# A decoder layer on one core: earlier loads, earlier fetches and a buffer ring for kept results alone in the seven-product part of the feed-forward projection

## The chip, the cores and the metric

The kernel runs on one core of a Trainium2 chip. The metric is the device time in microseconds (us) of one execution. Times of single instructions come from one profiled execution.

## The reference

The reference computes one hybrid decoder layer on 2048 tokens of width 1024 in float32: a combined projection, windowed attention and a convolution side by side, an output projection, and a SwiGLU feed-forward part with 2816 inner columns. Only the last part is touched by the change:

```python
h = h + rms_norm(mixed, mix_post_g)
hn = rms_norm(h, ffn_pre_g)
ff = (jax.nn.silu(hn @ w_gate) * (hn @ w_up)) @ w_down
h = h + rms_norm(ff, ffn_post_g)
```

## The kernel before

**Stages.** The 2048 tokens are cut into four tiles of 512. Letters after an @ in the profile name the stage: A the combined projection, B attention, C the convolution taps and their normalisation, U a folded weight, W the output projection, H the turned and split operands of the feed-forward part, F the gate and up projections, G the down projection and what belongs to it. F and G take two token tiles at once, so each runs twice, first for tiles 0 and 1 and then for 2 and 3. The order is: stage_pre (F), stage_p1 (F), stage_p2 (G), and the same again.

**Split operands.** A float32 product is made of three matmuls: each operand is split into a high part, which ScalarE copies in a rounded type (split_f, L824), and a low part, which VectorE (or GpSimd for some products of the second pass) gets by subtraction (lo). The third combination, low by low, is left out.

**Seven products.** For every pair of 128 inner columns the weight has four blocks A11, A12, A21, A22 (two weight rows of 128 x 1024, each cut in two), and the activations have four blocks B (two halves of the depth by two token tiles). Instead of eight block products the kernel makes seven, with sums of blocks (the list STEPS): number 0 is A11 by B11, 1 is S1 by T1, 2 is S2 by T2, 3 is A12 by B21, 4 is S3 by T3, 5 is S4 by B22, 6 is A22 by T4. A product is 12 matmuls of 128x128 by 128x512. The sums S1 to S4 are made from the weight blocks on VectorE in the function sums; T1 to T4 are made once by stage_h_sums. In the profile the operands of the first pass are named: T1 mid and mb, T2 ql, T3 p, T4 yt and mid, B22 hl.

**Kept results.** stage_pre makes products 0 and 3 ahead for the first PRES weight rows (20 of 22 in the first pass, 16 in the second) and puts product 0 into the DRAM tensor keeps. For such a row stage_p1 makes only products 1, 2, 4, 5 and 6, and adds product 2 onto the kept result: fetch (L1038) loads it into a tile of ring gb, and a ScalarE copy, the seed, (L1066) puts it into the bank "B".

**stage_p1.** It goes over 22 weight rows m (gate and up in turn), and in each over the products j = 0, 1, ... of that row (five or seven, nst in all). For every product it first splits the weight operand of the product three further on (AHEAD = 3), then makes the product, then empties the bank: product 1 is copied to the tile y5 (L1077) and product 2 to x2 (L1080), while their banks go on being added to. After product 4, y5 gets the bank "B" added by VectorE; after product 5, x2 gets the bank of product 5. For a gate row ScalarE then makes Silu of each (L1087); for an up row VectorE multiplies the gate's result by it, and the blocks and sums of blocks are stored in the DRAM tensor mids (L1094, L1100, L1103). At the end of a product's turn, at given j, stand the steps that the change moves: sums of the next row, fetch of the next row's kept result, and loads of the row after that, which loads one weight row into ring raw (L1006) and one into ring chl (L1008), 512 KB each.

**Rings.** A tile comes from a ring of a few buffers that goes by its tag (BUFS): gb has 2, at 2, raw 2, chl 5, fa 4, w 6. A new tile waits until the buffer's earlier tile has been read for the last time. In chl a row needs three tiles: its second weight row and two for S1 to S4. Ring at is also used by stage_p2 of the first pass for its first two operands (L1169).

**Order.** The text gives each instruction a priority by its place. A planner with its own estimates of time orders each engine's list, and SP's list of transfers, by what is ready and then by priority, and hands out the buffers; so an instruction can stand well ahead of its place in the text. Once planned, each list is executed in its order, and an instruction that waits holds what is behind it. Beside stage_p1 of the first pass run the w_down sums (stage_tsums: rings wx and fc, tensor td, lines L1119 and L1125) and the convolution taps.

## Time and profile before

| | |
|---|---|
| median of 3 runs | 1996.32 us (1993.41 to 1996.72) |
| the profiled execution | 1994.08 us, of which the span from first to last instruction is 1992.1 us |
| TensorE matmul busy | 1936.4 us (97%) |
| VectorE, ScalarE, GpSimd busy | 1467.2, 953.5, 247.2 us |
| moved by DMA | 444.06 MB, mean 223 GB/s |

Engines are named PE (matmul), PEld (weight load), DVE (VectorE), ACT (ScalarE), POOL (GpSimd), and SPq (SyncE's list of transfers). In a timeline row stand start, duration, engine, line, operation, out<-in, and in brackets how long the engine was idle before it and what ended that. Line 94 (L94) is the helper that records most VectorE operations and L85 the one that records matmuls, so these are told apart by their tiles.

### The profile page before, as it was taken

To read this page: it belongs to the slowest core of one execution; us is meant where nothing else is said; L and a number is where in the kernel's file an instruction comes from. 1 tells how busy PE (TensorE), PEld (TensorE's weight loads), DVE (VectorE), ACT (ScalarE), POOL (GpSimd) and SP (SyncE) were. 2 spreads that over 40 slices of the span, in tenths; PEclk is the share of its full clock that TensorE was granted. 3 is DMA by queue.
4 is the path that set the end of the run, shared out by engine and by line. 5 is a ranking of instruction groups with operands and counts; after the bars stand their busy time and mean duration, and the time that the engine had idled before them with its cause. 6 is when DMAs were issued, how large, how long until landed. Compare 5 with 4: busy or idle time off the path is not lost.

```text
span 1992.1 us, 26622 instructions
## 1 busy us (share of the span) xinstructions
PE 1936.4 (97%) x8730; PEld 1550.4 (78%) x8730; DVE 1467.2 (74%) x2648; ACT 953.5 (48%) x1878; POOL 247.2 (12%) x339
## 2 busy tenths in 40 slices
PE   8999999999998999899999999998899999999997
PEld 6877777777776878678888788886788888888886
DVE  4999969995875899777659964667766765455557
ACT  5455354447546533234355464656543433345443
POOL 4011111101121000000000110000023332311003
PEclk9999999999999999999999999999999999999999
DMA  8786657566659767865478787759845542466664
GB/s 307 252 305 218 210 187 257 182 214 216 225 199 322 258 222 254 280 231 190 143 238 273 255 270 243 253 201 376 289 147 170 169 159 85 142 227 197 211 195 143
DMA packets 224810, 444.06 MB, mean 223 GB/s; under 512 B 22136, under 2 KB 47904, under 8 KB 224672
## 3 DMA queue, kind: packets, MB, share of 16 engines
q1 hardware_dynamic: 212768, 429.79, 64.8%
q10 hardware_dynamic: 11904, 12.59, 1.8%
q8 instruction: 68, 1.11, 0.2%
q14 instruction: 70, 0.57, 0.1%
HBM read 327.46 MB, written 114.83 MB: 222 GB/s over the span
## 4 chain that ended last, share of the span: by engine, by line
PE 77%; DMA 11%; DVE 6%; issue 2%; ACT 2%; POOL 1%; SPq 1%; DVEq 0%; POOLq 0%; ACTq 0%
PE mm@F L85 29%; PE mm@G L85 18%; PE mm@A L85 14%; PE mm@W L85 5%; PE tr@B L85 4%; PE tr@W L85 3%; DMA gb@F<-keeps 1%; DMA chl@F<-w_gate 1%; DMA raw@F<-w_gate 1%; PE mm@U L85 1%; DMA chl@G<-h_scr 1%; DVE fc@C L94 1%; DVE w@F L94 1%; DMA td<-fc@G 1%; PE tr@B L492 1%
## 5 line engine op out<-in xcount | busy, mean ns | idle before, releaser
L94 DVE SCALAR_TENSOR_TENSOR fc@C<-glu@C,colt,fc@C 128x512 f32<-128x512 f32 x480 | 357.1, 758 | 2.8
L85 PE MATMUL mm@F<-hl@H,w@F 128*128 128x512 f32 x1056 | 256.8, 394 | 8.1 <-ACT mm@F L954 8.1
L85 PEld LDWEIGHTS mm@F<-hl@H,w@F 128*128 128x128 f32 x1056 | 200.4, 190 | 51.5 <-ACT mm@F L954 9.5
L85 PE MATMUL mm@G<-hl@G,hl@G 128*128 128x512 f32 x924 | 228.0, 392 | 1.8 <-DVE hl@G L94 1.6
L85 PE MATMUL mm@A<-hl@A,w@A 128*128 128x512 f32 x840 | 209.4, 397 | 4.4 <-ACT w@A L127 1.8
L85 PEld LDWEIGHTS mm@G<-hl@G,hl@G 128*128 128x128 f32 x924 | 171.7, 188 | 38.9 <-DVE hl@G L94 2.4
L824 ACT ACTIVATE w@F<-chl@F 128x512 fp32r<-128x512 f32 x220 | 134.8, 624 | 138.9 <-PE mm@F L85 131.4
L85 PE MATMUL mm@G<-w@G,hl@G 128*128 128x512 f32 x876 | 199.4, 389 | 0.0
L85 PEld LDWEIGHTS mm@G<-w@G,hl@G 128*128 128x128 f32 x876 | 164.4, 188 | 34.1
L85 PEld LDWEIGHTS mm@A<-hl@A,w@A 128*128 128x128 f32 x840 | 156.6, 189 | 43.1 <-issue 3.1
L94 DVE TENSOR_TENSOR w@F<-chl@F,w@F 128x512 fp32r<-128x512 f32 x198 | 145.6, 739 | 37.9 <-ACT w@F L824 37.3
L85 PE MATMUL mm@F<-mid@H,w@F 128*128 128x512 f32 x528 | 137.4, 408 | 12.5 <-ACT mm@F L954 10.6
L85 PE MATMUL mm@F<-ql@H,w@F 128*128 128x512 f32 x528 | 128.5, 391 | 6.8 <-ACT mm@F L1066 4.8
L85 PE MATMUL mm@F<-p@H,w@F 128*128 128x512 f32 x528 | 132.5, 397 | 0.0
L85 PEld LDWEIGHTS mm@F<-mid@H,w@F 128*128 128x128 f32 x528 | 103.7, 198 | 36.8 <-ACT mm@F L954 11.9
L85 PE MATMUL mm@F<-x@H,w@F 128*128 128x512 f32 x528 | 126.7, 391 | 0.0
L85 PEld LDWEIGHTS mm@F<-ql@H,w@F 128*128 128x128 f32 x528 | 98.9, 188 | 29.3 <-ACT mm@F L1066 6.2
L85 PEld LDWEIGHTS mm@F<-p@H,w@F 128*128 128x128 f32 x528 | 101.7, 193 | 21.8 <-ACT at@F L1080 0.2
L85 PEld LDWEIGHTS mm@F<-x@H,w@F 128*128 128x128 f32 x528 | 98.4, 188 | 21.1 <-issue 0.8
L127 ACT ACTIVATE w@A<-raw@A 128x512 fp32r<-128x512 f32 x110 | 67.5, 626 | 92.3 <-PE mm@A L85 63.5
L94 DVE TENSOR_TENSOR w@G<-raw@G,w@G 128x512 fp32r<-128x512 f32 x73 | 52.1, 714 | 68.8 <-ACT w@G L824 67.7
L495 POOL TENSOR_SCALAR_AFFINE_SELECT p@B<-p@B 128x512 f32<-128x512 f32 x62 | 52.9, 863 | 361.2 <-ACT p@B L493 359.8
(302 smaller groups left out, 3224.8 us busy)
## 6 DMA issues: line engine op xcount, KB each, us to landing
mids<-fa@F SPq DMA_DIRECT2D x154, 256.0 KB, 2.6
raw@A<-w_in SPq DMA_DIRECT2D x55, 512.0 KB, 4.5
w@A<-lo_in SPq DMA_DIRECT2D x84, 256.0 KB, 3.5
fc@G<-mids SPq DMA_DIRECT2D x77, 256.0 KB, 3.5
fa@G<-mids SPq DMA_DIRECT2D x75, 256.0 KB, 4.2
gb@F<-keeps SPq DMA_DIRECT2D x72, 256.0 KB, 4.5
w@W<-fold SPq DMA_DIRECT2D x32, 512.0 KB, 5.3
chl@F<-w_gate SPq DMA_DIRECT2D x22, 512.0 KB, 4.0
```

Source lines behind the costliest of these rows:

```text
L85: r = nc.tensor.matmul(*args, **kw)
L94: r = op(*args, **kw)
L127: act(w[:, 0], raw, AF.Copy)
L492: nc.tensor.transpose(o[:, i * P : (i + 1) * P], pr[:, 4 * g + i], ident)
L495: nc.gpsimd.affine_select(out=pg[:, kb].rearrange("p (i q) -> p i q", q=P), in_=pg[:, 1].rearrange("p (i q) -> p i q", q=P), compare_op=AL ...
L824: act(w[:, 0], x, AF.Copy)
```

## The change

Three edits in stage_p1. The tile y5 of product 1 comes from ring at instead of gb, so that gb holds kept results only, and y5 and x2 share the two buffers of at. The fetch of the next row's kept result moves from behind product j = nst - 2 to j = nst - 4, ahead of the sums of the next row. The loads of the row after the next move from the last product, j = nst - 1, to j = nst - 3. No instruction is added or taken away.

```diff
             elif i == 1:
-                y5 = f2("gb")
+                y5 = f2("at")
                 act(y5, o, AF.Copy)
...
             if j == nst - 4:
+                fetch(m + 1)
                 sums(m + 1)
-            if j == nst - 2:
-                fetch(m + 1)
-            if j == nst - 1:
+            if j == nst - 3:
                 loads(m + 2)
             yield 2.76
```

## The prediction

> **What bounds the kernel now.** I read the page first, then the busy time by stretch, the waits, and the timelines of single engines.

> ```profile
> span 1992.1 us, 26622 instructions
> PE 77%; DMA 11%; DVE 6%; issue 2%; ACT 2%; POOL 1%; SPq 1%; DVEq 0%; POOLq 0%; ACTq 0%
> ```

> The chain that ended last is TensorE for 77% and DMA for 11%: time can be won only where TensorE waits. The seven-product part (stage_p1) runs twice, from about 682 to 1022 us and from about 1439 to 1770 us. Its stretches, and within the first the four whose clock is below 1 (columns: PE, PEld, DVE, ACT, POOL busy, PEclk, DMA share, GB/s):

> ```profile
> 682.20:880.00 197.80, 184.13 (x769) 148.53 (x768) 167.57 (x271) 67.16 (x121) 0.00 (x0) 0.96 0.75 252
> 880.00:1005.68 125.68, 125.68 (x558) 104.03 (x556) 91.88 (x145) 50.82 (x90) 0.00 (x0) 1.00 0.51 163
> 1439.00:1767.00 328.00, 328.00 (x1449) 271.60 (x1448) 198.52 (x259) 129.12 (x229) 95.88 (x67) 1.00 0.44 146
> 696.00:706.00 10.00, 8.12 (x27) 6.19 (x28) 9.29 (x15) 4.26 (x9) 0.00 (x0) 0.83 0.81 258
> 829.00:836.00 7.00, 4.79 (x15) 3.62 (x14) 6.59 (x11) 0.00 (x0) 0.00 (x0) 0.76 0.89 284
> 838.00:847.00 9.00, 7.12 (x25) 5.26 (x24) 8.36 (x14) 3.31 (x6) 0.00 (x0) 0.81 0.71 261
> 870.00:882.00 12.00, 7.48 (x23) 5.75 (x22) 9.80 (x17) 2.79 (x5) 0.00 (x0) 0.72 0.71 259
> ```

> The second pass has no idle TensorE at all, nor has the first after 880 us: nothing is to be won there. From 682 to 880 us TensorE idles 197.80 - 184.13 = 13.7 us. It also loses clock after four of the gaps; window length times (1 - PEclk) gives 1.7, 1.7, 1.7 and 3.4, together 8.5 us. The whole pot is 22.2 us. Who ends the waits in that stretch (us in total, times, longest):

> ```profile
> PE mm@F L85 <- DVE gb@F L94: 5.0, 3, 2.2
> PE mm@F L85 <- ACT mm@F L1066: 4.8, 2, 4.5
> PE mm@F L85 <- ACT w@F L824: 1.9, 1, 1.9
> PE mm@F L85 <- ACT fa@F L1087: 1.0, 1, 1.0
> PE mm@F L85 <- DVE fa@F L94: 0.9, 1, 0.9
> ACT mm@F L1066 <- DMA gb@F<-keeps: 55.9, 11, 11.7
> DVE chl@F L94 <- DMA chl@F<-w_gate: 7.7, 5, 2.7
> DVE chl@F L94 <- DMA chl@F<-w_up: 7.4, 4, 4.1
> DVE wx@G L94 <- issue: 4.8, 3, 2.3
> DVE wx@G L94 <- DMA fc@G<-w_down: 4.5, 4, 1.8
> DVE wx@G L94 <- DMA wx@G<-w_down: 3.9, 2, 2.7
> ```

> ScalarE stands 55.9 us before the seed (L1066, which copies a kept result into a bank) because the kept result has not landed. VectorE stands 15.1 us for weight rows (chl) and 13.2 us for the w_down sums that run beside this stage. TensorE's 13.6 us split into 7.7 behind ScalarE and 5.9 behind VectorE.

> **The change, part by part.** First, what sets the issue of the moved transfers today:

> ```profile
> 882.01 0.63 ACT L1087 ACTIVATE fa@F<-gb@F 128x512 f32<-128x512 f32 x1 [0.69 <-DVE gb@F L94]
> 883.02 0.38 SPq L1038 DMA_DIRECT2D gb@F<-keeps  x1
> 857.57 0.60 ACT L1066 ACTIVATE mm@F<-gb@F 128x512 f32<-128x512 f32 x1 [2.47 <-DMA gb@F<-keeps]
> 895.33 0.33 SPq L1008 DMA_DIRECT2D chl@F<-w_gate  x1
> 896.64 0.60 ACT L1077 ACTIVATE gb@F<-mm@F 128x512 f32<-128x512 f32 x1 [2.02 <-PE mm@F L85]
> SPq L1008 <- DVE w@F L94: 8.8, 7, 3.6
> SPq L1006 <- DVE chl@F L94: 7.1, 10, 1.4
> ```

> *Ring of their own (gain).* The fetch for m = 14 is issued at 883.02, when the Silu at 882.01 has read the last of y5 of m = 12: kept results and y5 share the two buffers of gb, so a fetch waits for a y5. With gb to themselves, kept 14 needs only the buffer of kept 12, free once seed 12 (857.57) has run, at 858.2. The planner took 883.02 right behind its buffer, so I expect it to take the new place as early: up to 25 us sooner, where the longest wait for one was 11.7. I take all waits behind ScalarE as gone: 4.8 + 1.9 + 1.0 = 7.7 us of idle time (the ScalarE split at 841 and the Silu at 823 were late because they stand behind a waiting seed in ScalarE's order), and the clock lost after two of them, 1.7 (838:847) and 3.4 (870:882). Gain 12.8 us. What is late next is VectorE.

> [...]

> *Fetch two products earlier in the text.* On SP it moves ahead of a finished block's store (L1094) and of the block sums (L1100, L1103). The planner already issues out of the text's order, so with the buffer free this adds nothing of its own: 0. If it lands the fetch ahead of a store in SP's list, that store is late by one issue, 0.38 us, and nobody on the chain reads it before the next stage.

> *Weight rows two products sooner (about nothing).* The chl half of row m = 16 is issued at 895.33, about where y5 of m = 14 is copied (896.64), that is at j = 0 of m = 14, while the text puts it at j = 4; the new text says j = 2. It is already ahead of both. What holds it is its buffer: the L1008 and L1006 rows wait for VectorE to finish with an old tile (8.8 and 7.1 us). Five chl and two raw buffers remain, so the issue stays where it is. Indirectly it comes sooner: the VectorE split that frees the buffer follows a ScalarE split, which no longer stands behind a late seed. Of VectorE's part of the pot (5.9 idle plus clock 1.7 for 696:706 and 1.7 for 829:836, 9.3 in all) about half follows chl (15.1 of 28.3 us of its waits) and half w_down, which the change does not touch. I take 2 (bounds 0 and 9.3).

> *y5 moves into at, beside x2 (cost).* Two buffers now hold both, so y5 of m needs y5 or x2 of m - 1 read out. The trace of before has no such wait; its bound is how far each y5 copy came ahead of the first of those last reads. There are nine such copies in the first pass; first, last, and the one that matters:

> ```profile
> 697.01 0.58 ACT L1077 ACTIVATE gb@F<-mm@F 128x512 f32<-128x512 f32 x1
> 700.92 0.63 ACT L1087 ACTIVATE fa@F<-gb@F 128x512 f32<-128x512 f32 x1 [2.81 <-DVE gb@F L94]
> 965.09 0.60 ACT L1077 ACTIVATE gb@F<-mm@F 128x512 f32<-128x512 f32 x1 [0.32 <-PE mm@F L85]
> 966.10 0.62 ACT L1087 ACTIVATE fa@F<-gb@F 128x512 f32<-128x512 f32 x1
> 782.90 0.60 ACT L1077 ACTIVATE gb@F<-mm@F 128x512 f32<-128x512 f32 x1 [0.33 <-PE mm@F L85]
> 785.48 0.64 ACT L1087 ACTIVATE fa@F<-gb@F 128x512 f32<-128x512 f32 x1 [1.46 <-DVE gb@F L94]
> 784.91 2.88 PE L85 MATMUL mm@F<-hl@H,w@F 128*128 128x512 f32 x12
> ```

> The delays run from 701.55 - 697.01 = 4.5 us (first) to 966.72 - 965.09 = 1.6 (last); the nine add up to 28.2 us. Behind the copy stand later splits on ScalarE, and the S4 product (operand hl) on TensorE, which adds onto the bank that y5 is copied from. In eight of the nine the previous row's A22 product stands in between, which itself waits for that y5 sum, and S4 starts after the delayed copy would end. In the ninth the copy would end at 786.12 + 0.60 = 786.7, S4 began at 784.91: 1.8 us. I take 1.8; bounds 0 and 28.2. In the second pass TensorE has no gap to begin with and the order of these reads is the same: 0, with another 1.8 us (one late copy in a pass) as its bound.

> *The hand-over to the down projection (cost).* stage_p2 puts its first two operands into at as well:

> ```profile
> 1006.30 0.38 SPq L1169 DMA_DIRECT2D at@G<-mids  x1
> 1014.07 1.52 PE L85 MATMUL mm@G<-hl@G,hl@G 128*128 128x512 f32 x6
> 1015.42 2.43 PE L85 MATMUL tr@W<-w@W,ql@W 128*128 128x512 f32 x10
> 1017.03 0.69 DVE L94 TENSOR_TENSOR hl@G<-at@G,hl@G 128x512 fp32r<-128x512 f32 x1 [4.80 <-ACT hl@G L824]
> 1019.43 0.68 DVE L94 TENSOR_TENSOR fa@F<-fa@F,gb@F 128x512 f32<-128x512 f32 x1
> DMA to landing us min/median/max: 3.9/4.3/4.7
> ```

> Today they load from 1006.30 through the one buffer that x2 leaves. Afterwards the last y5 and x2 hold both, until 1020.1 in the old order, or 4.8 us sooner, 1015.3, since the y5 sum stood behind VectorE's wait of 4.80 for that very operand. With 4.3 to land and one split (0.63 by the ScalarE rows, 0.69 on VectorE) the first product of stage_p2 starts at 1020.9 to 1025.7 instead of 1014.07. To fill 1014 to then TensorE has the last row's A22 product (2.7) and the output projection's products beside it, ten of them in the row of 1015.42. Bounds 0 and 9 us (nothing but A22 to run); I take 2, as products of the output projection were ready there.

> **Sum.** 12.8 + 2 - 1.8 - 2 = 11.0 us. The profiled execution took 1994.08 us (2.0 around its span), so 1983.1; it lies 2.2 us below the median of the runs shown, 1996.32, which makes 1985.3, told as 1985.

> **The rivals.** *Given back:* the seeds are on time, but VectorE's waits for w_down (13.2 us) and the hand-over at its upper bound take the place. 12.8 - 1.8 - 9 = 2.0: 1994. For it: VectorE is busy 167.57 of 197.80 us, so little slack is left there. Against: nothing says that the output projection stops just then.

> *Slower, by the shared at ring:* the order is planned anew, and where the S4 product comes ahead of the previous A22 product, as at 784.91, each y5 delay reaches TensorE, through ScalarE's later splits too. If all 28.2 do: -14.8 + 28.2 + 2 = +15.4, or 2012; half of them is +1.3. It decides, with over 4 us lost, from about 17 of the 28 us on. Against: eight of nine are covered now, and the reads that delay y5 come sooner when VectorE waits less.

> *The transfers don't move:* if a fetch stays where it was in SP's list, behind waiting stores, nothing is won, and y5 and the hand-over cost 3.8: 2000. For it: SP's list is full between 682 and 880 us (DMA share 0.75). Against: the 883.02 issue follows its buffer at once.

> **How the numbers follow.** A measurement of this kernel tells about 0.2%, 4 us, from no change. I give the forecast 0.60, its own range being 1977 (VectorE's part mostly gained, no cost) to 1991 (half of the gain). Given back and unmoved transfers get 0.19, nearly all within 4 us, the slower rival 0.21, since a newly planned order has many places to go wrong. Faster is 0.62, same 0.17, slower 0.21. The range has to reach into the slower case, up to 2004: about 0.1 lies above it and less below 1977.

> **What would show it.** ScalarE's wait for keeps at L1066 falls from 55.9 us to under 10; each L1038 is issued at least 8 us ahead of its seed; TensorE's idle time from the start of stage_p1 to the end of the w_down sums falls from 13.7 to 4 to 6 us and the clock stays at 1 except once or twice; L1008 still waits for VectorE and keeps its place; the first at@G load follows the last y5 read. It would be wrong if L1077 waits for many microseconds in total and TensorE behind it, if a gap of over 4 us opens before the first product of stage_p2, or if the seeds still wait.

## The result, and the profile after

| | before | after |
|---|---|---|
| median | 1996.37 us (1993.41 to 1999.60, 7 runs) | 1988.14 us (1985.28 to 1992.01, 7 runs) |
| the profiled execution | 1994.08 us | 1987.34 us |
| its span | 1992.1 us | 1985.6 us |

The ratio is 0.996, 95% interval 0.9949 to 0.9971: the changed kernel is 8 us faster. The forecast was 1985. From the page of the changed kernel, its span and its chain; then, from the busy time by stretch, the same three stretches of stage_p1 (columns as before):

```profile
span 1985.6 us, 26616 instructions
...
PE 74%; DMA 12%; DVE 9%; issue 2%; ACT 2%; POOL 1%; SPq 0%; DVEq 0%; POOLq 0%; ACTq 0%
```

```profile
682.20:880.00 197.80, 185.33 (x807) 150.51 (x807) 173.88 (x282) 73.08 (x128) 0.00 (x0) 1.00 0.78 261
880.00:1005.68 125.68, 125.68 (x558) 104.12 (x557) 90.36 (x142) 51.13 (x91) 0.00 (x0) 1.00 0.51 166
1439.00:1767.00 328.00, 328.00 (x1448) 271.70 (x1447) 202.78 (x257) 127.95 (x225) 96.86 (x67) 1.00 0.44 149
```

In the first stretch TensorE makes 807 matmuls where it made 769, but its busy time hardly grew: it still idles 197.80 - 185.33 = 12.5 us, and the granted clock is 1.00 instead of 0.96. The chain shows VectorE with 9% instead of 6%. Who ends the waits in that stretch (us in total, times, longest):

```profile
ACT mm@F L1066 <- DMA gb@F<-keeps: 1.0, 1, 1.0
ACT mm@F L1066 <- DVE at@F L94: 43.1, 11, 8.4
PE mm@F L85 <- DVE at@F L94: 8.1, 5, 3.0
PE mm@F L85 <- DVE fa@F L94: 4.3, 2, 3.0
ACT at@F L1077 <- DVE fa@F L94: 2.6, 2, 1.9
ACT at@F L1080 <- DVE fa@F L94: 5.2, 5, 1.7
```

The seed's wait for its kept result is gone (55.9 to 1.0 us). In its place the seed waits 43.1 us for VectorE's sums, which empty banks. TensorE waits for nobody but VectorE. In the timeline, two of its gaps with what stands before them on VectorE:

```profile
827.10 0.69 DVE L94 TENSOR_TENSOR wx@G<-fc@G,wx@G 128x512 f32<-128x512 f32 x1 [3.50 <-DMA fc@G<-w_down]
827.71 0.68 DVE L94 TENSOR_TENSOR at@F<-at@F,mm@F 128x512 f32<-128x512 f32 x1
828.44 1.66 PE L85 MATMUL mm@F<-yt@H,w@F 128*128 128x512 f32 x6 [2.97 <-DVE at@F L94]
...
867.32 0.69 DVE L94 TENSOR_TENSOR chl@F<-chl@F 128x512 f32<-128x512 f32 x1 [2.42 <-DMA chl@F<-w_gate]
870.00 1.66 PE L85 MATMUL mm@F<-mid@H,w@F 128*128 128x512 f32 x6 [3.03 <-DVE fa@F L94]
```

VectorE stands 3.50 us for a w_down block, or 2.42 us for a weight row, and the sum or product that would free TensorE's bank is queued behind that.

To see where the time came from I cut each trace at three products: the first S1 by T1 product (operand mb) and the last A22 product (operand yt) of the first pass, and the first A22 product of the second. The first pass took 334.12 us before and 325.07 after, a difference of 9.05. From there to the second pass it is 435.29 and 435.80, the second pass 318.01 in both, the tail 219.75 and 219.49. Ahead of the first pass, where the change touches nothing, the profiled run of after happened to be 2.3 us slower. So in these two runs the whole gain is in the first pass.

### The profile page after: what moved, and what is told of

Its sections match the earlier page's. It is cut to its first block, busy times and chain, and to the rows that moved or that the text cites. A ratio compares the mean times of both kernels' runs of the same rounds, so it can differ in the third digit from the quotient of the medians.

```text
span 1985.6 us, 26616 instructions
## 1 busy us (share of the span) xinstructions
PE 1930.0 (97%) x8730; PEld 1546.9 (78%) x8730; DVE 1468.7 (74%) x2648; ACT 957.5 (48%) x1878; POOL 245.1 (12%) x339
## 4 chain that ended last, share of the span: by engine, by line
PE 74%; DMA 12%; DVE 9%; issue 2%; ACT 2%; POOL 1%; SPq 0%; DVEq 0%; POOLq 0%; ACTq 0%
PE mm@F L85 29%; PE mm@G L85 16%; PE mm@A L85 14%; PE mm@W L85 5%; PE tr@B L85 4%; PE tr@W L85 2%; DVE fc@C L94 2%; PE mm@U L85 1%; DVE w@F L94 1%; DVE chl@F L94 1%; DMA raw@F<-w_gate 1%; DMA raw@F<-w_up 1%; DMA td<-wx@G 1%; PE tr@B L492 1%; DMA chl@G<-h_scr 1%
## 5 line engine op out<-in xcount | busy, mean ns | idle before, releaser
L94 DVE SCALAR_TENSOR_TENSOR fc@C<-glu@C,colt,fc@C 128x512 f32<-128x512 f32 x480 | 357.2, 758 | 2.8
L85 PE MATMUL mm@F<-hl@H,w@F 128*128 128x512 f32 x1056 | 257.7, 396 | 7.9 <-ACT mm@F L954 7.9
L85 PEld LDWEIGHTS mm@F<-hl@H,w@F 128*128 128x128 f32 x1056 | 201.2, 191 | 51.4 <-ACT mm@F L954 9.2
L85 PE MATMUL mm@G<-hl@G,hl@G 128*128 128x512 f32 x924 | 227.4, 393 | 1.9 <-DVE hl@G L94 1.9
L824 ACT ACTIVATE w@F<-chl@F 128x512 fp32r<-128x512 f32 x220 | 135.8, 625 | 166.4 <-PE mm@F L85 161.3
L85 PE MATMUL mm@A<-hl@A,w@A 128*128 128x512 f32 x840 | 208.0, 395 | 5.4 <-ACT w@A L127 2.6
L85 PEld LDWEIGHTS mm@G<-hl@G,hl@G 128*128 128x128 f32 x924 | 171.7, 188 | 38.3 <-DVE hl@G L94 2.7
L85 PE MATMUL mm@G<-w@G,hl@G 128*128 128x512 f32 x876 | 199.4, 389 | 0.0
L85 PEld LDWEIGHTS mm@G<-w@G,hl@G 128*128 128x128 f32 x876 | 164.5, 188 | 34.1
L85 PEld LDWEIGHTS mm@A<-hl@A,w@A 128*128 128x128 f32 x840 | 155.5, 188 | 43.8 <-ACT w@A L127 3.3
L94 DVE TENSOR_TENSOR w@F<-chl@F,w@F 128x512 fp32r<-128x512 f32 x198 | 146.9, 745 | 30.4 <-ACT w@F L824 29.9
L85 PE MATMUL mm@F<-mid@H,w@F 128*128 128x512 f32 x528 | 137.6, 408 | 14.0 <-ACT mm@F L954 9.7
L85 PEld LDWEIGHTS mm@F<-mid@H,w@F 128*128 128x128 f32 x528 | 103.6, 198 | 38.5 <-ACT mm@F L954 11.3
L85 PE MATMUL mm@F<-p@H,w@F 128*128 128x512 f32 x528 | 129.1, 390 | 0.1
L85 PE MATMUL mm@F<-ql@H,w@F 128*128 128x512 f32 x528 | 127.8, 389 | 0.0
L85 PE MATMUL mm@F<-x@H,w@F 128*128 128x512 f32 x528 | 126.9, 392 | 0.0
L85 PEld LDWEIGHTS mm@F<-p@H,w@F 128*128 128x128 f32 x528 | 99.1, 188 | 21.0 <-ACT at@F L1080 0.5
L85 PEld LDWEIGHTS mm@F<-ql@H,w@F 128*128 128x128 f32 x528 | 99.1, 188 | 20.5
L85 PEld LDWEIGHTS mm@F<-x@H,w@F 128*128 128x128 f32 x528 | 98.5, 188 | 21.0 <-issue 0.8
L94 DVE TENSOR_TENSOR w@G<-raw@G,w@G 128x512 fp32r<-128x512 f32 x73 | 52.2, 715 | 68.6 <-ACT w@G L824 67.6
```

Of the source, the lines that this page charges most:

```text
L85: r = nc.tensor.matmul(*args, **kw)
L94: r = op(*args, **kw)
L824: act(w[:, 0], x, AF.Copy)
```

## The experiments

The first pass of each kernel's profiled run, with TensorE's idle time in it summed by what ended it from the timeline rows ("rest" is what is left of the pass beyond some 312 us of work and the idle time; the time lost to a lower clock, 8.5 us in the profiled run of before, makes it up within 1.2 us, except with three gb buffers, where it is 3.4 of the 5.8). The ratio is to the kernel before on the same chip:

| kernel | ratio, 95% interval | pass | behind ScalarE | behind VectorE | rest |
|---|---|---|---|---|---|
| *y5 and kept share gb* | | | | | |
| before | 1 | 334.12 | 7.7 | 5.9 | 8.6 |
| loads only | 1.0002 [0.9993, 1.0010] | 330.73 | 6.6 | 5.7 | 6.4 |
| fetch place only | 1.0003 [0.9994, 1.0011] | 333.53 | 10.2 | 5.1 | 6.3 |
| room only | 1.0005 [0.9992, 1.0019] | 334.90 | 9.8 | 7.0 | 6.1 |
| three gb buffers | 0.9887 [0.9869, 0.9905] | 329.28 | 6.4 | 5.2 | 5.8 |
| *y5 and kept apart* | | | | | |
| after | 0.9960 [0.9949, 0.9971] | 325.07 | 0 | 12.4 | 0.7 |
| ring only | 0.9956 [0.9941, 0.9972] | 330.05 | 0 | 12.4 | 5.6 |
| ring and fetch | 0.9944 [0.9932, 0.9957] | 327.08 | 0 | 10.8 | 4.3 |
| kept in at, moved places | 0.9944 [0.9930, 0.9959] | 320.85 | 2.9 | 4.4 | 1.6 |
| kept in at, old places | 0.9936 [0.9918, 0.9954] | 319.73 | 1.9 | 4.0 | 1.9 |
| after, three at buffers | 0.9989 [0.9976, 1.0001] | 331.97 | 5.0 | 10.5 | 4.6 |

My theory was that a kept result is fetched late because its buffer hangs on y5, and that the late seed is what costs. The rivals were the two moved places in the text.

Some of these kernels execute the same lists. Laid side by side by operation and tile (without buffer numbers), from the first instruction to the last, the lists of all four engines and SP's list of transfers are in loads only, fetch only and room only (the control of three gb buffers) those of before. Ring and fetch has the lists of the whole change, ring only differs from it in five places of VectorE's list and five of SP's, and the two kernels with the kept result in at have the same lists. So the rows of one order show how far its profiled runs lie apart: the pass took 330.73 to 334.90 us in the four of before's order, and 325.07 and 327.08 us in the two of the change's.

### The change in parts

Ring only: y5 in at, fetch and loads at their old places.

```diff
-                y5 = f2("gb")
+                y5 = f2("at")
```

> Only y5 moves from ring gb to ring at; fetch and loads keep their old places in the text. Theory (the shared ring held the fetches): the whole gain of about 8 us stays, ratio 0.995 to 0.997 to the kernel before; ScalarE's wait for keeps at L1066 falls from 55.9 us to under 5, and each fetch is issued about 20 us ahead of its seed. Rival (the place in the text matters): with the old place the fetch is still late, less than half of the gain, ratio over 0.998.

Loads only:

```diff
-            if j == nst - 1:
+            if j == nst - 3:
                 loads(m + 2)
```

> Only loads moves, from j = nst - 1 to j = nst - 3; y5 and the fetch stay as before. Theory (the loads are held by their buffers, not by the text): no change, ratio 0.999 to 1.001, L1008 for row m + 2 still issued about when y5 of row m is copied. Rival (weight rows arrive sooner): VectorE's 15.1 us of waits for chl fall to under 5 and 2 to 9 us are won, ratio 0.9955 to 0.999.

Fetch place only:

```diff
             if j == nst - 4:
+                fetch(m + 1)
                 sums(m + 1)
-            if j == nst - 2:
-                fetch(m + 1)
```

> Only fetch moves, to j = nst - 4 ahead of sums; y5 stays in gb. Theory: the fetch still waits for a y5 to be read out, no change, ratio 0.999 to 1.001, ScalarE's wait for keeps stays over 40 us. Rival: its earlier place alone brings it in time, ratio under 0.998.

Ring and fetch: both of these edits, without the loads.

> The change without its loads part: y5 in ring at and fetch at j = nst - 4, loads at j = nst - 1. Theory: as the whole change, ratio 0.995 to 0.997. Rival (loads carry part of the gain): 2 us or more behind the whole change, ratio 0.9975 or more.

Measured: ring only 1990.67 us, loads only 1997.76, fetch place only 1998.51, ring and fetch 1986.33, against 1997.85 for before on that chip. ScalarE's wait at the seed in the same stretch, for ring only, loads only and fetch place only:

```profile
ACT mm@F L1066 <- DMA gb@F<-keeps: 1.5, 1, 1.5
```

```profile
ACT mm@F L1066 <- DMA gb@F<-keeps: 52.1, 12, 13.1
```

```profile
ACT mm@F L1066 <- DMA gb@F<-keeps: 56.9, 12, 13.2
```

The ring carries the gain. The two moves alone do nothing, because the planner makes the same lists with them as without: with y5 and the kept results in gb the fetch is issued a median of 4.9 us ahead of its seed in both runs (5.2 in before); with y5 in at it is 26 us, also from the old place. Once the ring is split, the loads' move changes nothing in the lists either, and the fetch's move next to nothing; the intervals of ring only, ring and fetch, and the whole change overlap.

### Kept results late, but apart from y5

Kept in at: the kept result moves into at beside x2, y5 stays alone in gb, fetch and loads at their new places. Against the changed kernel:

```diff
 (stage_p1, fetch)
-                kept[m] = f2("gb")
+                kept[m] = f2("at")
...
-                y5 = f2("at")
+                y5 = f2("gb")
```

> The change with the two rings exchanged: y5 stays alone in gb, and in stage_p1 the kept results share at with x2 (fetch and loads at their new places). Theory (a fetch is late because its ring also holds a tile that is read out late): x2 is read out as late as y5, so the fetch waits again, ScalarE's wait for keeps stays over 35 us, ratio 0.999 to 1.001 to the kernel before. Rival (any new order of the lists brings the gain): ratio under 0.998.

Here I was wrong. It took 1984.78 us, ratio 0.9944, the full gain, though the seeds wait nearly as long in total as before. The rival's ratio came true. The same ring with fetch and loads at their old places, so that only the ring is changed:

> The kernel before with one edit: in stage_p1 the kept result comes from ring at, which it shares with x2, and y5 stays alone in ring gb; fetch and loads stay at their old places, behind j = nst - 2 and j = nst - 1. Theory A (what counts is only that the kept result and y5 do not share two buffers, because y5 is read late and is written right after the seed): 0.994 to 0.9965 of before, as the run with the kept result in at and the two moved places, and ScalarE's wait for keeps at L1066 may still be 40 us or more. Rival B (that run gained by its early fetch and loads, since here the kept result is fetched only behind x2's last read): 0.999 to 1.001, with ScalarE's wait at 50 us and TensorE idle of 6 us or more behind L1066 in 682 to 880 us.

It took 1984.03 us against 1997.76, ratio 0.9936, just below theory A's range and far from B's; as its lists are those of the run before it, it measures that order a second time. Its waits in the stretch from 682 to 880 us, the stretch itself, and from the timeline a fetch with its seed:

```profile
ACT mm@F L1066 <- DMA at@F<-keeps: 45.4, 12, 6.5
PE mm@F L85 <- ACT mm@F L1066: 1.9, 2, 1.6
```

```profile
682.20:880.00 197.80, 191.96 (x833) 156.62 (x832) 176.17 (x286) 73.94 (x132) 0.00 (x0) 0.99 0.78 260
```

```profile
777.30 0.49 SPq L1038 DMA_DIRECT2D at@F<-keeps  x1
782.40 0.60 ACT L1066 ACTIVATE mm@F<-at@F 128x512 f32<-128x512 f32 x1 [3.83 <-DMA at@F<-keeps]
```

The fetch is issued 5.1 us ahead of its seed, no sooner than before, and ScalarE waits 45.4 us. Yet TensorE idles only 197.80 - 191.96 = 5.8 us, the least of all. So ScalarE's wait in total is not what costs; a long single wait may be: the longest is 6.5 us here and 8.1 in the run before this one, against 11.7 before and 13.1 to 13.2 in the two runs that gained nothing. What holds is that each kernel that split the ring and changed nothing else beside the places was faster, and none that left it shared with two buffers. But those that were faster also have newly planned lists, in which TensorE's matmuls too stand in another order than before, while those that left the ring shared with two buffers and gained nothing kept before's lists. No run changes the buffers and holds the order. So whether the free buffer pays, or the order that is planned with it, isn't shown, and neither is why kept results go better with x2 than with y5. A new order alone is no gain: the third at buffer below brings one too.

### VectorE's waits for w_down

The block subtractions of the w_down sums are left out of the changed kernel, so that blocks are loaded and stored as they are.

```diff
-                vtt(o, p_, q_, ALU.subtract)
```

> The change with the 44 subtractions of the w_down sums left out (the blocks are loaded and stored as they are, so the transfers stay). Theory (after the change TensorE's 12.4 us of idle time in the first pass come from VectorE, and there mostly from its 13 us of waits for w_down): the idle time from 682 to 880 us falls under 6 us, ratio to the kernel before 0.990 to 0.994. Rival (VectorE is late through the chl waits): idle time stays over 9 us, ratio 0.994 or more.

1984.57 us, ratio 0.9941 [0.9928, 0.9954], no more than ring and fetch, with 11.0 us of idle left. The w_down waits turned into waits for weight rows, by the waits of the same stretch and the largest gap of its timeline:

```profile
DVE chl@F L94 <- DMA chl@F<-w_gate: 17.2, 6, 6.9
DVE chl@F L94 <- DMA chl@F<-w_up: 10.8, 7, 3.9
```

```profile
786.02 2.93 PE L85 MATMUL mm@F<-mid@H,w@F 128*128 128x512 f32 x6 [6.79 <-DVE fa@F L94]
```

My theory that w_down costs most of the remaining idle time fell: VectorE is fed by loads, and takes the next late one. Then the subtractions on GpSimd instead of VectorE:

```diff
-                vtt(o, p_, q_, ALU.subtract)
+                ptt(o, p_, q_, ALU.subtract)
```

> The change with the 44 subtractions of the w_down sums on GpSimd, which is idle in that pass, in place of VectorE. Theory: as with the subtractions left out, 3 to 8 us faster than the whole change, ratio to the kernel before 0.990 to 0.9945. Rival (GpSimd slows VectorE's instructions beside it, as in the second pass where a VectorE product took 1.78 us in place of 0.68): no gain over the whole change, ratio 0.996 or more.

2005.09 us, ratio 1.0039 [1.0026, 1.0052]: slower than before. The stretch, and its waits:

```profile
682.20:880.00 197.80, 173.24 (x723) 139.48 (x723) 167.98 (x220) 64.40 (x115) 66.01 (x40) 0.95 0.72 242
```

```profile
POOL wx@G L1123 <- DMA wx@G<-w_down: 62.4, 9, 11.0
PE mm@F L85 <- DVE fa@F L94: 17.3, 4, 9.1
```

One subtraction takes 66.01 / 40 = 1.65 us on GpSimd and 0.69 on VectorE (the 827.10 row). TensorE waits 17.3 us for VectorE's block sums and products where it waited 4.3, though VectorE has 40 subtractions less in this stretch. The rival is what the trace shows; from its timeline a GpSimd subtraction and a VectorE split beside it, which takes 0.69 us elsewhere:

```profile
691.24 1.62 POOL L1123 TENSOR_TENSOR wx@G<-fc@G,wx@G 128x512 f32<-128x512 f32 x1
691.63 1.77 DVE L94 TENSOR_TENSOR w@F<-chl@F,w@F 128x512 fp32r<-128x512 f32 x1
```

In this stretch 33 of VectorE's instructions took over 0.8 us, up to 1.78, and each of them overlaps a GpSimd subtraction; in the changed kernel none took over 0.75. By an estimate from these rows they took 31 us more together, which is more than the 40 x 0.69 = 28 us that VectorE was spared. VectorE's instructions that read a bank (mm) kept 0.67 to 0.69 us beside GpSimd's.

### The shared at ring and the hand-over

The first two operands of stage_p2 from fa instead of at, in the changed kernel:

```diff
-                rawa[i] = f2("fc" if last else "at" if i < 2 else "fa")
+                rawa[i] = f2("fc" if last else "fa")
```

> The change with the first two operands of stage_p2 (first pass) taken from ring fa instead of at, so that y5 and x2 don't hold them up. Theory (the output projection's products fill the hand-over): as the whole change, ratio 0.995 to 0.997. Rival (the later start costs the 2 us or more that the prediction allowed): 2 to 5 us faster than the whole change, ratio 0.993 to 0.9945.

1991.61 us, ratio 0.9979 [0.9967, 0.9991]: no gain over the whole change, so the hand-over was not costing anything that this could win back. Its lists are in yet another order; why that gave up part of the gain isn't shown. Then a third buffer for y5 and x2, with room made for it:

```diff
-    BUFS = dict(... gb=2, ... at=2, ...)
+    BUFS = dict(... gb=2, ... at=3, ...)
...
-        return sb.tile([P, 8], dt, tag="sm" + kind, name=nm("sm"), bufs=16)[:, 0:n]
+        return sb.tile([P, 8], dt, tag="sm" + kind, name=nm("sm"), bufs=8)[:, 0:n]
...
-    junk = cst.tile([P, D], BF16, name="junk")
+    junk = cst.tile([P, D], I8, name="junk")
...
-        g = t_("glu", (P, 576))[:, 0 : HALO + T]
+        g = t_("glu", (P, HALO + T))[:, 0 : HALO + T]
...
-                        gbs.append(t_("glu", (P, 576))[:, 0:T])
+                        gbs.append(t_("glu", (P, HALO + T))[:, 0:T])
```

> The changed kernel with a third buffer in ring at, made possible by the same three savings. Theory A (in the changed kernel y5 and x2 hold each other in two buffers: ScalarE's waits at L1077 and L1080 of 7.8 us and part of TensorE's 12.4 us of idle time come from there): both waits near 0, idle at 5 to 9 us, 0.991 to 0.994 of before, faster than the changed kernel by some 3 to 8 us. Rival B (what TensorE waits for in the changed kernel is VectorE's list, with its waits for loads): idle at 10 to 14 us, 0.9945 to 0.9965 of before.

1994.60 us, ratio 0.9989 [0.9976, 1.0001]: neither theory had that. The copies of y5 and x2 no longer wait for a buffer, as theory A said, but the idle time did not fall, as B said, and most of the gain went. A new wait came up, in the timeline:

```profile
820.28 0.63 ACT L1087 ACTIVATE fa@F<-at@F 128x512 f32<-128x512 f32 x1 [3.71 <-DMA mids<-fa@F]
820.82 0.58 ACT L1066 ACTIVATE mm@F<-gb@F 128x512 f32<-128x512 f32 x1
821.34 0.58 ACT L1077 ACTIVATE at@F<-mm@F 128x512 f32<-128x512 f32 x1
821.97 3.04 PE L85 MATMUL mm@F<-hl@H,w@F 128*128 128x512 f32 x12 [2.32 <-ACT at@F L1077]
```

The Silu at 820.28 waited 3.71 us for a store to free its fa tile, and the seed and the y5 copy stood behind it in ScalarE's list; the S4 product waits for that copy. With two buffers each copy had waited a little; with three it stands behind something else.

### A third gb buffer

The same room, on the kernel before, spent on gb: y5 and kept results share three buffers. With it, its control, which has the room and does not spend it.

```diff
-    BUFS = dict(... gb=2, ... at=2, ...)
+    BUFS = dict(... gb=3, ... at=2, ...)
```

> The kernel before with a third buffer in ring gb, still shared by kept results and y5; room is made by a narrower dump tile for squares, fewer buffers for the row statistics and a glu tile of its exact width. Theory A (a buffer that is free in time is what lacked; sharing as such does no harm): the fetch is issued about one product or more earlier, ScalarE's wait for keeps falls below 15 us and the time is 0.994 to 0.9965 of before. Rival B (the two kinds of tile hold each other up in any ring of theirs, because a fetch still queues behind a late read of y5): wait above 30 us and 0.9985 to 1.001.

> The kernel before with nothing but the three savings of room (a narrower dump tile for squares, eight instead of sixteen buffers for row statistics, a glu tile of its exact width): the control of the two kernels with a third buffer. Expected 0.999 to 1.001 of before; a difference beyond that has to be taken off theirs.

The control took 1999.45 us, no change. The third gb buffer took 1973.90 us, ratio 0.9887 [0.9869, 0.9905]: the fastest of all, beyond what either theory gave. But the fetch is still issued a median of 4.9 us ahead of its seed, and the seeds still wait, in the same stretch:

```profile
ACT mm@F L1066 <- DMA gb@F<-keeps: 32.3, 9, 8.8
```

Of the 21.4 us between its span and the control's (1995.0 to 1973.6), 5.6 are in the first pass, 8.7 ahead of it and 7.0 between the passes. There stands stage_pre, which has a fetch and a seed of its own (L937, L954) in the same ring. TensorE's wait for that seed ahead of the first pass and between the passes, in the kernel before, and then with three buffers:

```profile
PE mm@F L85 <- ACT mm@F L954: 8.1, 4, 3.7
PE mm@F L85 <- ACT mm@F L954: 10.6, 4, 4.1
```

```profile
PE mm@F L85 <- ACT mm@F L954: 2.8, 3, 1.2
PE mm@F L85 <- ACT mm@F L954: 6.0, 2, 5.0
```

Together 18.7 us became 8.8. So in these runs the third buffer saved more around stage_pre than in the part that the change touches. The clock came back with the idle time: the mean granted clock was 0.994 or 0.995 in all five runs, against 0.985 to 0.990 in before's 23 on that chip. This kernel's lists are newly planned as well. Split rings and a third gb buffer together were not tried.

## Why the prediction was right, and where it was not

**Right: where nothing would move.** The second pass took 318.01 us before and after. The two moves in the text brought nothing by themselves: the planner made the same lists with them, as was expected of one that already issues out of the text's order. The load of row 12 still goes out beside the y5 copy of row 10, and a fetch behind the seed that frees its buffer. From the timeline of the changed kernel:

```profile
727.65 0.60 ACT L1066 ACTIVATE mm@F<-gb@F 128x512 f32<-128x512 f32 x1 [1.89 <-DVE at@F L94]
728.67 0.38 SPq L1038 DMA_DIRECT2D gb@F<-keeps  x1
...
754.27 0.60 ACT L1066 ACTIVATE mm@F<-gb@F 128x512 f32<-128x512 f32 x1 [0.66 <-DVE at@F L94]
...
830.82 0.60 ACT L1077 ACTIVATE at@F<-mm@F 128x512 f32<-128x512 f32 x1
831.08 0.39 SPq L1008 DMA_DIRECT2D chl@F<-w_gate  x1
```

A fetch now goes out right behind the seed of two rows earlier, 728.67, and its own seed runs at 754.27: 25.6 us ahead. The median is 26 where it was 5.2, so some 20 us sooner, within the "up to 25 us sooner" of the prediction.

**Right in size, but given back: the seeds' 7.7 us of idle time.** TensorE's idle time behind ScalarE fell from 7.7 us (6.6 to 10.2 in the other profiled runs of before's lists) to 0. Idle time in all was to fall to 4 to 6 us, and fell only from 13.6 to 12.4.

**The step that failed: VectorE.** "What is late next is VectorE" was right, but I priced it at a gain of 2 us within bounds of 0 and 9.3, and left out that it could get worse. TensorE's idle time behind VectorE rose from 5.9 to 12.4 us, and the other runs bear it out: 5.1 to 7.0 in those of before's lists, 10.8 and 12.4 in ring and fetch and ring only. So the rival "given back" was half true: VectorE's waits took the seeds' place, but the hand-over, from which its sum took 9 us, cost nothing. The late seeds may have hidden VectorE's lateness, but that isn't shown: with kept results in at VectorE's part is only 4 us. The bound should have reached below zero, since VectorE was busy 167.57 of 197.80 us and fed by loads.

**The clock.** I counted 5.1 us of clock with the seeds and left the rest in VectorE's part. In the profiled run all of it, some 8 us, came back, and that carries most of the 9.05 us of that run. That was luck (the last section shows what it hung on): ring and fetch has the same lists and 5.1 us of clock lost in its profiled pass, and ring only has the same 12.4 us of idle time and a rest of 5.6 us. All runs together tell more. A run's span times one minus its mean granted clock estimates what the clock cost it; the mean is 21.6 us over the seven runs of the changed kernel, 18.2 and 21.9 over the six each of ring and fetch and of ring only, and 25.5 to 26.0 for the 65 runs of before on the three chips of the experiments. So the clock gave back some 4 to 8 us, around the 5.1 that I counted with the seeds. The sum of 11.0 came out near 8 with terms that were off in both directions, VectorE some 8 us too good and the costs of 3.8 us not there; that it came so near is in part luck.

**The theory behind the ring.** The edit was the right one, but "the seeds are on time, so TensorE goes on" is not the needed cause: with kept results in at the fetch stays late and the gain is as large. What that kernel and the changed one share is that y5 and the kept result no longer use the same two buffers, and that their lists are newly planned.

**The costs.** The shared at ring made the copies wait 7.8 us (L1080 and L1077), but TensorE never behind them; I had 1.8. The hand-over cost nothing where I had 2: the loads went out behind the last y5 and x2 reads as expected, and the output projection filled the time, as the timeline has it:

```profile
1008.49 0.68 DVE L94 TENSOR_TENSOR fa@F<-fa@F,at@F 128x512 f32<-128x512 f32 x1
1009.57 1.21 SPq L1168 DMA_DIRECT2D at@G<-mids  x2
1015.02 3.11 PE L85 MATMUL tr@W<-w@W,ql@W 128*128 128x512 f32 x13
1017.97 1.30 PE L85 MATMUL mm@G<-hl@G,hl@G 128*128 128x512 f32 x5
```

**What stays open:** why kept results beside x2 leave VectorE's part at 4 us and y5 beside x2 at 11 to 12; and how much of the gain is the free buffer and how much the order that was planned with it.

## What to carry to other kernels

Where a planner orders the lists, see first whether an edit changes them at all: here two of three edits did not, and where a tile that is fetched ahead shared a small ring with one that is read late, the ring was the thing to change. Look for the same wait under other lines of the same ring, since a buffer more helped there too. An engine that waits 45 us in total may hold up the bounding engine for only 2: count only where the bounding engine stands behind it, and expect the next engine in its chain, here a VectorE fed by loads, to take over part of that idle time. Price that engine's part on both sides of zero.

## What the runs showed of the hardware

The length of a gap alone did not decide whether the clock was lowered. In the changed kernel gaps of 2.97 and 3.03 us left it at 1.00 over the whole stretch. In ring only a gap of 2.81 us was followed by 0.50:

```profile
716.95 1.54 PE L85 MATMUL mm@F<-yt@H,w@F 128*128 128x512 f32 x4 [2.81 <-DVE at@F L94]
```

```profile
714.18:717.59 3.41, 0.64 (x3) 0.55 (x4) 3.41 (x7) 1.21 (x3) 0.00 (x0) 1.00 0.93 296
717.60:721.01 3.41, 3.41 (x10) 2.63 (x9) 3.41 (x6) 1.64 (x3) 0.00 (x0) 0.50 0.96 339
```

```profile
823.98:827.40 3.42, 1.50 (x7) 0.92 (x5) 0.30 (x1) 0.00 (x0) 0.00 (x0) 1.00 0.65 214
827.40:830.81 3.41, 2.37 (x10) 1.99 (x11) 3.41 (x7) 1.15 (x2) 0.00 (x0) 1.00 0.63 252
830.81:834.22 3.41, 3.41 (x16) 2.82 (x16) 3.05 (x5) 2.10 (x4) 0.00 (x0) 1.00 0.67 190
```

The first gap leaves TensorE idle for 2.77 us of one beat, and the next beat runs at 0.50, which by an estimate loses 3.41 x 0.50 = 1.7 us. The second is cut by the beat into 1.92 and 1.04 us, and the clock stays at 1.00. From 682 to 1010 us the traces of before and of the changed kernel have 187 beats at 1.00. The two with the most idle time, 2.86 and 2.20 us, both in before, were each followed by one at 0.50. Of the four with 1.80 to 1.93 us the two of before (1.88 and 1.80) were, and the two of the changed kernel (1.93 and 1.84) were not; of the 181 with 1.63 us or less none was. So before's gaps of 1.80, 1.88 and 2.21 us were followed by 0.50, and the changed kernel's of 2.97 and 3.03 us were not.
